# Memory attention: probabilities times values as float32 products that write to one partition half, instead of split products with a fold

## The chip, the cores and the metric

The kernel runs on one core of one Trainium2 chip. The metric is device time in microseconds: the time of the core from start to end of one execution, the median of three runs. The profile is of one further execution, in which each engine's instructions are recorded: PE (matmuls; PEld is its weight load), DVE (VectorE), ACT (ScalarE), POOL (GpSimd), and SP, which issues most DMAs.

## What is computed

Two layers of an encoder on 1024 tokens of width 1024, all in float32. A layer mixes tokens in three groups (Fourier, window attention, memory attention), projects, and runs a SwiGLU block. The change touches the memory attention alone: 4 heads of 64 channels attend to 256 memory rows.

```python
def _memory_attn(q, km, vm):
    b, s, _, _ = q.shape
    scores = jnp.einsum('bshd,bmhd->bhsm', q, km).astype(jnp.float32) * (HEAD_DIM ** -0.5)
    probs = jax.nn.softmax(scores, axis=-1)
    out = jnp.einsum('bhsm,bmhd->bshd', probs.astype(vm.dtype), vm)
    return out.reshape(b, s, MEM_WIDTH)
```

## The kernel before

Operands of most matmuls are split: `split` (lines 149 to 152) writes a rounded copy `hi` (type fp32r, on ACT, line 151) and the rest `lo = src - hi` (on DVE or POOL, line 152), and a product is the sum of hi x hi, hi x lo, lo x hi. A few matmuls take float32 operands directly; one of them is the second half of the window attention (line 773), where two products write to partitions 0 to 63 and 64 to 127 of one tile.

Memory attention in a layer is eight units, one for each of 4 heads and 2 halves of the tokens (512 each). A unit has three steps, and `mem_units` (line 879) runs scores of unit i, values of unit i - 2 and the turn of unit i - 1 together:

- `mem_scores` (829): 16 matmuls `ms` of 256 columns, row maxima on DVE (842), exponentials on ACT (846), the division on POOL (852);
- `mem_turn` (857): 8 transposes `mpT` on PE, and for each of the two blocks of 128 memory rows a `split` of the 128x512 probabilities: one ACT copy and one DVE subtraction;
- `mem_values` (868): 4 matmuls `mav` of 512 columns. The stationary operand holds the head's 64 channels of V twice, the rounded part for partitions 0 to 63 and the rest for 64 to 127, so the tile holds two partial sums. ACT copies one to the head's partition half of `ym` (876), DVE adds the other (877).

`Memory.load` (455) reads K and V of the layer back from DRAM (`kvd`, one DMA), makes the stacked K (`dup_stack`) and splits V.

The program weaves these units with the q projection (`qp`, with the transposes `qT`), and with `load_wout`, which loads 256 KB pieces of the output weights through three buffers (`raws`) and splits each with one ACT (910) and one DVE instruction (911); it needs the buffers of the q weights, so it begins when the q projection ends. After the memory attention come the output product of the Fourier and memory groups (`mo`) and the window attention (`sc`, `pT`, `av`). A scheduler then fixes each engine's order; at run time every engine goes through its own list in that order and waits where an operand is not there.

Of the kernel before, what the change touches and what calls it, by code (L numbers as in the profile page):

```python
# [12 lines left out]
F32R = mybir.dt.float32r  # L13
# [3 lines left out]
ALU = mybir.AluOpType  # L17
# [8 lines left out]
HD = 64  # L26
# [42 lines left out]
def tile_encoder(ctx: ExitStack, tc: tile.TileContext, T, C, out):  # L69
    nc = tc.nc  # L70
# [24 lines left out]
    def shaped(ap, shape):  # L95
        names = "abcde"[: len(shape)]
        dims = {c: d for c, d in zip(names, shape)}
        return ap.rearrange(f"p ({' '.join(names)}) -> p {' '.join(names)}", **dims) if len(shape) > 1 else ap

    def at(k, *shape, dt=F32):  # L100

        o = int(k * 256)
        ap = arenas[F32R if dt is F32R else F32][:, o : o + math.prod(shape)]
        return shaped(ap.bitcast(dt) if dt is I32 else ap, shape)
# [16 lines left out]
    def run(k, n, step):  # L121
        return Ring(*[k + i * step for i in range(n)])
# [9 lines left out]
    ras, rbs, bsums, xs_ = run(40, 3, 2), run(46, 6, 2), Ring(58, 32, 34), Ring(36, 24)  # L132

    zzs, dhs, tabs = run(112, 2, 4), run(64, 2, 4), run(72, 4, 2)
    mps, phs, yys = run(24, 2, 4), run(16, 3, 4), run(104, 2, 4)
    wcs, abs_ = Ring(112, 116, 96, 100, 48, 52, 56, 60), Ring(80)

    def sm(n, name="v"):
# [4 lines left out]
    def ps(shape, name="ps", tag="pd"):  # L143
        return psp[tag].tile([P] + list(shape), F32, tag=tag, name=nm(name))

    f32 = lambda ap: ap.bitcast(F32)
    mm = nc.tensor.matmul

    def split(hi, lo, src, lo_eng=None):

        nc.scalar.copy(hi, src)  # L151
        return (lo_eng or nc.vector).tensor_tensor(out=lo, in0=src, in1=f32(hi), op=ALU.subtract)  # L152
# [16 lines left out]
    def cst(*shape):  # L169
# [20 lines left out]
        out=mask[:, 0:P], in_=mask[:, 0:P], pattern=[[1, P]], compare_op=ALU.is_ge,  # L190
# [4 lines left out]
        out=mask[:, 2 * P : 3 * P], in_=mask[:, 2 * P : 3 * P], pattern=[[-1, P]],  # L195
# [179 lines left out]
    def dup_stack(kh, kl, src, j):  # L375

        r = slice(64 * j, 64 * j + 64)
        o = slice(64 - 64 * j, 128 - 64 * j)
        nc.scalar.copy(kh[r], src[r])
        nc.scalar.copy(kh[o], src[r])  # L380
        nc.vector.tensor_tensor(out=kl[r], in0=src[r], in1=f32(kh[r]), op=ALU.subtract)
        nc.vector.tensor_tensor(out=kl[o], in0=src[r], in1=f32(kh[r]), op=ALU.subtract)
# [9 lines left out]
    class Memory:  # L392
# [60 lines left out]
            nc.sync.dma_start(kvd[self.l], at(self.ks, 1024))  # L453

        def load(self):
            raw = at(32, 4, 256)
            nc.sync.dma_start(raw, kvd[self.l].rearrange("p (i c) -> p i c", i=4))
            self.km = [at(16 + 4 * i, 2, 2, NMEM, dt=F32R) for i in range(2)]
            self.vm = at(120, 2, 4, 2, HD, dt=F32R)
            for ci in range(2):  # L460
                for j in range(2):
                    dup_stack(self.km[ci][:, j, 0], self.km[ci][:, j, 1], raw[:, ci], j)
            v = raw[:, 2:4].rearrange("p t (h d) -> p t h d", h=4)
            for mt in range(2):
                split(self.vm[:, mt, :, 0, :], self.vm[:, mt, :, 1, :], v[:, mt])


    class Mix:
# [388 lines left out]
        def mem_turn(self, e):  # L857
            res = []
            for mt in range(2):
                pT = ps([4, P], "mpT", "pT")  # L860
                for b in range(4):
                    nc.tensor.transpose(pT[:, b, :], e[b // 2][:, b % 2, mt * P : mt * P + P], ident)
                pp = mps(2, 512, dt=F32R)
                split(pp[:, 0], pp[:, 1], pT.rearrange("p h q -> p (h q)"))
                res.append((pp[:, 0], pp[:, 1]))
            return res

        def mem_values(self, h, half, pp):
            av = ps([512], "mav", "av")
            for mt in range(2):  # L870
                lhs = self.mem.vm[:, mt, h].rearrange("p a d -> p (a d)")
                for i in range(2):
                    mm(av, lhs, pp[mt][i], start=mt == 0 and i == 0, stop=mt == 1 and i == 1)
            s = h % 2
            d = self.ym[half][64 * s : 64 * s + 64, h // 2, :]
            nc.scalar.copy(d, av[64:128])
            nc.vector.tensor_tensor(out=d, in0=av[0:64], in1=d, op=ALU.add)

        def mem_units(self):
            todo = [(h, half) for half in range(2) for h in range(4)]  # L880
# [401 lines left out]
    kvd = drp.tile([DEPTH, P, 1024], F32, name="kvd")  # L1282
# [34 lines left out]
    for l in range(DEPTH):  # L1317
# [4 lines left out]
        q = mix.skewed(mix.q, mix.q_turn, NT)  # L1322
# [132 lines left out]
```

## Time and profile before

| | |
|---|---|
| median of 3 runs | 2135.3 us (2132.69 to 2136.14) |
| the profiled execution's own time | 2135.5 us |
| its span, first to last instruction | 2133.7 us |
| busy: PE, DVE, ACT, POOL | 2013.2, 1577.7, 1060.6, 863.4 us |
| mean granted TensorE clock | 0.969 of full |

Busy time is the union of an engine's instructions; a share of the span is an average over stages with different limits, so the stage that changes has to be read by itself. The memory attention lies at about 141 to 228 us (layer 0) and 1200 to 1284 us (layer 1).

### The profile page before, as it was taken

How to read it: one execution, taken by the hardware profiler on the slowest of the kernel's cores; microseconds unless marked ns; L12 is line 12 of the kernel's file. 1: busy time of each engine (PE TensorE's matmuls, PEld its weight loads, DVE VectorE, ACT ScalarE, POOL GpSimd, SP SyncE). 2: the span in 40 equal slices, each digit the busy share in tenths (PEclk: the TensorE clock that was granted, in tenths of full speed). 3: DMA queues.
4: the chain of work that ended last, by engine and by line, in shares of the span. 5: the costliest groups of instructions: out<-in, count | busy, mean ns of one | idle time of the engine just before them, and what ended most of it. 6: DMA issues, size and time to landing. Idle time of an engine off the chain costs nothing.

```text
span 2133.7 us, 28334 instructions
## 1 busy us (share of the span) xinstructions
PE 2013.2 (94%) x9490; PEld 1655.0 (78%) x9490; DVE 1577.7 (74%) x2441; ACT 1060.6 (50%) x2257; POOL 863.4 (40%) x858
## 2 busy tenths in 40 slices
PE   7998999699999999999989989996999999999997
PEld 6887887478888887878868768775888888878785
DVE  7568756898877877657875686578987787876774
ACT  6467776553333334444544677776433333345441
POOL 4244446653423434213453444475442333431322
PEclk9998999899999999999989989998999999999998
DMA  6112123422332326968731122243232232378874
GB/s 221 45 50 65 65 94 105 152 65 94 118 101 95 112 94 194 318 221 287 246 138 41 60 64 85 75 137 110 84 129 94 94 111 92 123 249 284 276 261 138
DMA packets 173602, 287.50 MB, mean 135 GB/s; under 512 B 15480, under 2 KB 73360, under 8 KB 173456
## 3 DMA queue, kind: packets, MB, share of 16 engines
q1 hardware_dynamic: 165392, 266.82, 38.1%
q10 hardware_dynamic: 8064, 18.88, 2.3%
q8 instruction: 74, 1.21, 0.2%
q14 instruction: 72, 0.59, 0.1%
HBM read 219.06 MB, written 66.58 MB: 134 GB/s over the span
## 4 chain that ended last, share of the span: by engine, by line
PE 74%; DMA 8%; DVE 7%; ACT 4%; POOL 4%; issue 2%; SPq 0%; POOLq 0%; DVEq 0%; ACTq 0%
PE fo L1232 12%; PE qz L1104 11%; PE qx L1104 11%; PE qy L1104 11%; PE mo L162 7%; PE qw L1104 5%; PE kvp L162 4%; PE qp L162 3%; DVE arena_r L152 3%; DMA arena_f<-actd 2%; PE sc L728 2%; PE pT L765 2%; DMA arena_f<-in_w_ffn_out 1%; ACT arena_r L151 1%; PE zT L162 1%
## 5 line engine op out<-in xcount | busy, mean ns | idle before, releaser
L151 ACT CAST arena_r<-arena_f 128x512 fp32r<-128x512 f32 (+1 forms) x780 | 443.1, 591 | 674.0 <-PE qz L1104 115.5
L152 DVE TENSOR_TENSOR arena_r<-arena_f,arena_r 128x512 fp32r<-128x512 f32 (+1 forms) x676 | 536.6, 816 | 182.9 <-ACT arena_r L151 179.6
L1232 PE MATMUL fo<-arena_r 128*128 128x512 f32 x1848 | 432.2, 395 | 17.5 <-ACT arena_r L151 15.1
L1232 PEld LDWEIGHTS fo<-arena_r 128*128 128x128 f32 x1848 | 351.7, 191 | 94.6 <-ACT arena_r L151 17.7
L1104 PE MATMUL qy<-arena_r 128*128 128x512 f32 x1056 | 261.5, 397 | 27.6 <-ACT arena_r L151 16.5
L1104 PEld LDWEIGHTS qy<-arena_r 128*128 128x128 f32 x1056 | 201.5, 192 | 72.0 <-ACT arena_r L151 17.0
L1094 DVE TENSOR_TENSOR arena_f<-arena_f 128x512 f32<-128x512 f32 x220 | 206.0, 939 | 5.1
L1104 PE MATMUL qz<-arena_r 128*128 128x512 f32 x704 | 196.3, 389 | 1.8 <-DVE arena_r L152 1.8
L1124 POOL TENSOR_TENSOR arena_f<-arena_f 128x512 f32<-128x512 f32 x44 | 73.0, 1658 | 292.8 <-ACT arena_f L1109 292.8
L1216 POOL TENSOR_TENSOR arena_f<-arena_f 128x512 f32<-128x512 f32 x50 | 73.6, 1475 | 269.5 <-DVE arena_r L152 136.2
L1104 PEld LDWEIGHTS qz<-arena_r 128*128 128x128 f32 x704 | 132.0, 188 | 29.8 <-DVE arena_r L152 2.4
L1156 POOL TENSOR_TENSOR arena_f<-arena_f 128x512 f32<-128x512 f32 x44 | 73.6, 1674 | 165.6 <-DVE arena_f L1136 119.1
L152 POOL TENSOR_TENSOR arena_r<-arena_f,arena_r 128x256 fp32r<-128x256 f32 (+2 forms) x104 | 88.8, 859 | 118.4 <-ACT arena_r L151 93.3
L1104 PE MATMUL qx<-arena_r 128*128 128x512 f32 x528 | 127.7, 389 | 1.4 <-ACT arena_r L151 1.4
L1104 PE MATMUL qw<-arena_r 128*128 128x512 f32 x528 | 127.6, 389 | 0.0
L1104 PE MATMUL qx<-big,arena_r 128*128 128x512 f32 x528 | 126.8, 389 | 0.0
L1104 PEld LDWEIGHTS qx<-arena_r 128*128 128x128 f32 x528 | 99.1, 188 | 22.5 <-ACT arena_r L151 2.0
L1104 PE MATMUL qz<-big,arena_r 128*128 128x512 f32 x352 | 115.5, 389 | 0.0
L1104 PEld LDWEIGHTS qw<-arena_r 128*128 128x128 f32 x528 | 99.1, 188 | 20.8
L1104 PEld LDWEIGHTS qx<-big,arena_r 128*128 128x128 f32 x528 | 99.1, 188 | 20.6
L162 PE MATMUL mo<-arena_r 128*128 128x512 f32 x384 | 102.6, 406 | 5.5 <-POOL arena_r L152 4.0
L162 PE MATMUL mo<-big,arena_r 128*128 128x512 f32 x384 | 102.3, 404 | 0.0
(223 smaller groups left out, 3558.1 us busy)
## 6 DMA issues: line engine op xcount, KB each, us to landing
arena_f<-in_w_ffn_out SPq DMA_DIRECT2D x264, 256.0 KB, 4.3
arena_f<-in_w_ffn_in SPq DMA_DIRECT2D x88, 512.0 KB, 3.6
actd<-arena_f SPq DMA_DIRECT2D x154, 256.0 KB, 3.7
arena_f<-actd SPq DMA_DIRECT2D x154, 256.0 KB, 4.2
arena_f<-in_w_in SPq DMA_DIRECT2D x40, 256.0 KB, 2.7
arena_f<-in_x SPq DMA_DIRECT2D x16, 512.0 KB, 4.1
arena_f<-in_w_out SPq DMA_DIRECT2D x32, 256.0 KB, 2.8
pmd<-arena_f ACTq DMA_DIRECT2D x32, 256.0 KB, 2.0
```

The source lines that it names most:

```text
L151: nc.scalar.copy(hi, src)
L152: return (lo_eng or nc.vector).tensor_tensor(out=lo, in0=src, in1=f32(hi), op=ALU.subtract)
L162: mm(self.dst, a, b, start=self.i == 0, stop=self.i == self.n - 1)
L728: mm(pt, lhs, self.kst[g][i][:, k0 * P : k1 * P], start=i == 0, stop=i == 1)
L765: nc.tensor.transpose(pT[:, h, :], es_[h // 2][:, h % 2, j * P : j * P + P], ident)
L1094: nc.vector.tensor_tensor(out=s, in0=a, in1=b, op=op)
L1104: mm(pt, a, b, start=start and n == 0, stop=n == 11, skip_group_check=not start)
L1124: nc.gpsimd.tensor_tensor(out=self.v, in0=self.v, in1=self.s2, op=ALU.add)
L1156: (G if i in (0, 3) else V).tensor_tensor(out=a[i], in0=c, in1=g[i], op=ALU.mult)
L1216: (nc.vector, nc.gpsimd)[k % 2].tensor_tensor(out=s, in0=x, in1=y, op=op)
L1232: mm(pt, ab[:, 0, x, sl], ab[:, 1, y], start=new and first and j == 0, stop=last and j == 2, skip_group_check=not new)
```

## The change

V stays in float32: `Memory.load` fetches K and V with two DMAs into two places and no longer splits V. `mem_turn` copies each turned block of probabilities once (ACT, float32) into one of four buffers `mps` in place of a split into one of two. `mem_values` makes two float32 products of 64 x 512 a head in place of four split ones of 128 x 512; they write straight to the partition half that the head has in `ym`, and one ACT copy moves it there. What goes: two DVE subtractions and one DVE addition a unit, and V's split (two ACT, two DVE instructions a layer).

```diff
-    mps, phs, yys = run(24, 2, 4), run(16, 3, 4), run(104, 2, 4)
+    mps, phs, yys = Ring(14, 56, 58, 10), run(16, 3, 4), run(104, 2, 4)
...
-            raw = at(32, 4, 256)
-            nc.sync.dma_start(raw, kvd[self.l].rearrange("p (i c) -> p i c", i=4))
+            raw, v = at(32, 2, 256), at(12, 2, 256)
+            kv = kvd[self.l].rearrange("p (i c) -> p i c", i=4)
+            nc.sync.dma_start(raw, kv[:, 0:2])
+            nc.sync.dma_start(v, kv[:, 2:4])
...
-            v = raw[:, 2:4].rearrange("p t (h d) -> p t h d", h=4)
-            for mt in range(2):
-                split(self.vm[:, mt, :, 0, :], self.vm[:, mt, :, 1, :], v[:, mt])
...
-                pp = mps(2, 512, dt=F32R)
-                split(pp[:, 0], pp[:, 1], pT.rearrange("p h q -> p (h q)"))
-                res.append((pp[:, 0], pp[:, 1]))
+                pf = mps(512)
+                nc.scalar.copy(pf, pT.rearrange("p h q -> p (h q)"))
+                res.append(pf)
...
-        def mem_values(self, h, half, pp):
+        def mem_values(self, h, half, pf):
+
+            r = slice(64 * (h % 2), 64 * (h % 2) + 64)
             av = ps([512], "mav", "av")
             for mt in range(2):
-                lhs = self.mem.vm[:, mt, h].rearrange("p a d -> p (a d)")
-                for i in range(2):
-                    mm(av, lhs, pp[mt][i], start=mt == 0 and i == 0, stop=mt == 1 and i == 1)
-            s = h % 2
-            d = self.ym[half][64 * s : 64 * s + 64, h // 2, :]
-            nc.scalar.copy(d, av[64:128])
-            nc.vector.tensor_tensor(out=d, in0=av[0:64], in1=d, op=ALU.add)
+                mm(av[r], self.mem.vm[:, mt, h], pf[mt], start=mt == 0, stop=mt == 1)
+            nc.scalar.copy(self.ym[half][r, h // 2, :], av[r])
```

The scheduler orders all engines anew. First place: PE in layer 0, the second unit's values (`mav_1709` before, `mav_1699` after) among the q projection's matmuls `qp`. Before:

```order
L162 MATMUL qp_1863<-big_1252,arena_r 128x512 x2
L873 MATMUL mav_1709<-arena_r 128x512
L162 MATMUL qp_1863<-big_1252,arena_r 128x512 x2
L840 MATMUL ms_1694<-arena_r 128x256 x4
L873 MATMUL mav_1709<-arena_r 128x512 x3
L862 MATMUL mpT_1716<-const,arena_f 128x128 x3
```

After:

```order
L162 MATMUL qp_1838<-big_1252,arena_r 128x512
L872 MATMUL mav_1699<-arena_f 64x512
L162 MATMUL qp_1838<-big_1252,arena_r 128x512
L872 MATMUL mav_1699<-arena_f 64x512
L162 MATMUL qp_1838<-big_1252,arena_r 128x512 x3
L839 MATMUL ms_1675<-arena_r 128x256 x4
```

Four matmuls of 128 columns out became two of 64, each alone between matmuls of the whole array. The same holds for the third unit, whose two products stand around the last `qp` of the layer.

Second place: DVE in layer 0, just after the q projection, where the weight splits (L911 before, L907 after) run. Before:

```order
L911 SCALAR_TENSOR_TENSOR big_2010<-arena_f,const,big_2010 128x512
L877 TENSOR_TENSOR arena_f<-mav_1794,arena_f 64x512
L152 TENSOR_TENSOR arena_r<-mpT_1801,arena_r 128x512
L152 TENSOR_TENSOR arena_r<-mpT_1808,arena_r 128x512
L843 TENSOR_SCALAR nmx_1768<-rmax_1767 128x2
L842 TENSOR_REDUCE rmax_1815<-ms_1818 128x2
L911 SCALAR_TENSOR_TENSOR big_2010<-arena_f,const,big_2010 128x512
```

After:

```order
L907 SCALAR_TENSOR_TENSOR big_1975<-arena_f,const,big_1975 128x512
L842 TENSOR_SCALAR nmx_1753<-rmax_1752 128x2
L907 SCALAR_TENSOR_TENSOR big_1975<-arena_f,const,big_1975 128x512
L842 TENSOR_SCALAR nmx_1753<-rmax_1752 128x2
L389 TENSOR_TENSOR arena_r<-qT_1866,arena_r 64x4x128
L841 TENSOR_REDUCE rmax_1795<-ms_1798 128x2
```

The two subtractions and the addition of a unit are gone from between the weight splits; nothing else took their place.

Third place: PE in layer 0, the values of the last two units at the end of the memory attention (`sc` and `pT` are the window attention's). Before:

```order
L728 MATMUL sc_2194<-arena_r 128x384 x2
L728 MATMUL sc_2198<-arena_r 128x384 x2
L728 MATMUL sc_2298<-arena_r 128x384 x2
L873 MATMUL mav_2054<-arena_r 128x512
L925 MATMUL ssp_2103<-const,arena_f 128x2 x2
L873 MATMUL mav_2054<-arena_r 128x512 x3
```

After:

```order
L872 MATMUL mav_1989<-arena_f 64x512
L727 MATMUL sc_2143<-arena_r 128x384 x2
L727 MATMUL sc_2147<-arena_r 128x384 x2
L861 MATMUL mpT_1993<-const,arena_f 128x128
L861 MATMUL mpT_1999<-const,arena_f 128x128
L861 MATMUL mpT_1993<-const,arena_f 128x128
L861 MATMUL mpT_1999<-const,arena_f 128x128
L764 MATMUL pT_2120<-const,arena_f 128x128 x4
L872 MATMUL mav_2014<-arena_f 64x512
```

The products of two neighbouring heads, which write to different partition halves, stand apart from each other; nowhere in the list do two heads' products follow one another.

## Rows read from the trace of the kernel before

**Rows 1.** The page: span, then busy time, share and instructions of three engines.

```profile
span 2133.7 us, 28334 instructions
PE 2013.2 (94%) x9490; PEld 1655.0 (78%) x9490; DVE 1577.7 (74%) x2441; ACT 1060.6 (50%) x2257; POOL 863.4 (40%) x858
```

**Rows 2.** Busy time by stretch: length, then PE, PEld, DVE, ACT, POOL, clock, DMA.

```profile
core 0: us, PE busy (x) PEld busy (x) DVE busy (x) ACT busy (x) POOL busy (x), PEclk, DMA share, GB/s
141.00:179.00 38.00, 38.00 (x202) 32.19 (x201) 30.09 (x56) 17.67 (x47) 14.64 (x20) 1.00 0.00 1
180.00:222.00 42.00, 33.05 (x154) 26.36 (x152) 38.88 (x80) 34.74 (x88) 16.14 (x26) 0.80 0.26 82
222.00:230.00 8.00, 7.74 (x29) 6.97 (x30) 3.87 (x17) 5.27 (x19) 3.83 (x7) 0.57 0.00 1
1240.00:1284.00 44.00, 35.99 (x167) 27.15 (x165) 39.72 (x89) 35.93 (x94) 18.61 (x28) 0.84 0.25 78
1284.00:1292.00 8.00, 7.81 (x40) 6.40 (x41) 5.84 (x17) 6.78 (x20) 5.70 (x11) 1.00 0.19 69
```

**Rows 3.** The chain that ended last, 158 to 181 us: start, length, what.

```profile
164.63 5.03 PE qp L162 x22
...
176.54 0.93 PE qp L162 x4
177.47 0.23 PE mav L873
...
178.63 0.71 PE mav L873 x3
...
179.37 0.59 ACT arena_f L876
...
179.97 1.02 ACT arena_f L846 x4
```

**Rows 4.** Line 773's float32 matmuls: count, shortest, median and longest ns.

```profile
L773 PE MATMUL av<-big,arena_f x176: 379/379/431, 306.7 to 1440.9; 128*64 128x256 f32 x176
```

**Rows 5.** Timeline of PE around line 773: start, length, count of records.

```profile
306.40 0.40 PE L162 MATMUL mo<-arena_r 128*128 128x512 f32 x1
306.73 0.44 PE L773 MATMUL av<-big,arena_f 128*64 128x256 f32 x2
...
306.73 0.65 PE L773 MATMUL av<-big,arena_f 128*64 128x256 f32 x4
...
307.00 0.39 PE L773 MATMUL av<-big,arena_f 128*64 128x256 f32 x2
307.31 0.27 PE L925 MATMUL ssp<-const,arena_f 128*128 128x2 f32 x1
...
323.71 1.08 PE L773 MATMUL av<-big,arena_f 128*64 128x256 f32 x8
```

**Rows 6.** Busy time by stretch of the instructions on `mpT`: PE, PEld, DVE, ACT.

```profile
180.00:222.00 42.00, 8.11 (x42) 5.98 (x40) 7.85 (x12) 6.65 (x12) 0.80 0.26 82
1240.00:1284.00 44.00, 8.57 (x40) 5.66 (x40) 8.06 (x12) 6.65 (x12) 0.84 0.25 78
```

**Rows 7.** The same for line 877, DVE alone.

```profile
180.00:222.00 42.00, 4.08 (x6) 0.80 0.26 82
1240.00:1284.00 44.00, 4.18 (x7) 0.84 0.25 78
```

**Rows 8.** What SP's queue waited for, 100 to 230 us: total, times, longest.

```profile
SPq L909 <- DVE big L911: 57.2, 8, 47.5
```

**Rows 9.** The load of K and V, and the group with V's rounded copies.

```profile
L457 SPq DMA_DIRECT2D arena_f<-kvd x2: 339/339/339, 97.7 to 1160.0; - x2
...
DMA to landing us min/median/max: 3.2/3.2/3.2
...
L151 ACT CAST arena_r<-arena_f 128x256 fp32r<-128x256 f32 x84 | 33.2, 404 | 25.5 <-PE mo L162 10.3 <-PE ms L840 5.8 <-PE yfp L162 3.8
```

More of the change, by code (lines that the diff above doesn't have):

```diff
@@ L455, in load @@
         def load(self):
-            raw = at(32, 4, 256)
-            nc.sync.dma_start(raw, kvd[self.l].rearrange("p (i c) -> p i c", i=4))
+            raw, v = at(32, 2, 256), at(12, 2, 256)
+            kv = kvd[self.l].rearrange("p (i c) -> p i c", i=4)
+            nc.sync.dma_start(raw, kv[:, 0:2])
+            nc.sync.dma_start(v, kv[:, 2:4])
             self.km = [at(16 + 4 * i, 2, 2, NMEM, dt=F32R) for i in range(2)]
-            self.vm = at(120, 2, 4, 2, HD, dt=F32R)
+            self.vm = v.rearrange("p t (h d) -> p t h d", h=4)
             for ci in range(2):
```

## The prediction, made before the changed kernel was run

> **What bounds the kernel now.** The page comes first: PE is busy for 2013.2 of 2133.7 us, DVE for 1577.7, ACT for 1060.6 [rows 1]. By that alone, work taken from DVE is worth nothing. But the memory attention is only two stretches of some 85 us, so the second view is busy time by stretch, cut there. It shows two regimes in each layer. From 141 to 179 us PE is busy for all of 38.00 us at full clock and DVE for 30.09: the q projection runs there, and two units' values lie among its matmuls. From 180 to 222 us the picture turns over: DVE is busy for 38.88 of 42.00, ACT for 34.74, PE for 33.05 at a mean granted clock of 0.80, a mix of its 1.2 and 2.4 GHz levels. Layer 1 repeats it at 1240 to 1284 us: DVE 39.72 of 44.00, ACT 35.93, PE 35.99 at 0.84 [rows 2]. The third view, the chain that ended last, confirms the border: up to 179.3 us every link is PE, and then it goes over to ACT (the copy L876, the exponentials L846) [rows 3]. So the change is read twice: what PE pays in the first stretch, where everything waits for it, and what DVE gives back in the second, where it is the fullest engine.
>
> **What a head costs PE.** Now: four matmuls of 512 columns. The chain gives 22 of that size 5.03 us, 0.229 each, and three `mav` 0.71 [rows 3], so a head is 0.92 us. The new products, float32 with 64 columns out, are not in the memory attention's trace, but line 773 has the form with 256 columns. Its 176 records belong to 88 products (22 key blocks a layer, two halves, two layers), so a product is two records [rows 4]. Eight records take 1.08 us, four 0.65 [rows 5]: four more, that is one product to each partition half, add 0.43. There are two readings. If the two halves run side by side, each product takes the whole 0.43 for 256 columns, 0.86 for 512. If the records run one after another, a product is 0.22 for 256 and 0.43 for 512. In a window of 20 ns the timeline already shows two records begun at 306.73 [rows 5], where one after another would put 0.11 between them; I take 0.86 and keep 0.43 as the lower end.
>
> Going over to such a matmul and back costs too: from the last `mo` at 306.40 to the first record at 306.73 is 0.33 where 0.23 is usual, and from the last pair at 307.00, which streams for 0.215, to the next matmul at 307.31 another 0.10 is lost [rows 5]. A head with both products together is then 2 x 0.86 + 0.2 = 1.92 us, and 2.12 where other matmuls stand between them, as at the first place of the order. Against 0.92 that is 1.0 to 1.2 more, 1.1 in the mean; by the lower reading 0.14 to 0.34.
>
> One rule of the skill would make this cheaper. Line 773's pairs start together [rows 5], but in the new order two heads' products nowhere stand side by side. The Trainium skill, TensorEngine Tiling (Array Packing), section Key Properties, says that different tiles of the array can load weights and multiply in parallel. By that rule a pair of neighbouring heads would cost what one does, if the order brought them together; it does not, so the sum goes without it, and it stands below as a rival.
>
> **The first stretch: a loss.** In the new order the first two units' values lie among the `qp` as before, and the third's two products stand around the last of them. PE has no gap there. Two heads at 1.1 and half of the third make 2.8 us a layer, 5.6 in all. By the lower reading it is 1.2; with the third in full and split, 1.0 + 1.2 + 1.2 = 3.4 a layer, 6.8.
>
> **The second stretch: a gain.** DVE loses the subtractions, 7.85 us in layer 0 and 8.06 in layer 1 [rows 6], and the additions, 4.08 and 4.18 [rows 7]: 11.9 of its 38.88 and 12.2 of its 39.72. It falls to 27 and 27.5 and bounds no more. Next is ACT, whose copies stay as many and as large: 34.74 and 35.93. DVE as the bound filled 0.926 and 0.903 of the stretches. If ACT does as well, the stretches shrink to 34.74 / 0.926 = 37.5 and 35.93 / 0.903 = 39.8 us: gains of 4.5 and 4.2. What can keep ACT below that is its supply of output weights: SP's loads L909 waited for DVE's L911 for 57.2 us in total [rows 8] (47.5 of it in one wait, for the end of the q projection), and a DVE that comes sooner to L911 frees those buffers sooner. The two pull against each other, so I take the same shares, 8.7 in all. Bounds: nothing, if another engine fills the stretch; at ACT 0.95, 5.4 and 6.2, 11.6 in all.
>
> **The clock.** From 222 to 230 us PE is busy for 7.74 of 8.00 at a clock of 0.57, while the same place of layer 1 (1284 to 1292) has 1.00 [rows 2]. Before that, PE had stood idle for 9 of 42 us. Most of these 8 us are work at half speed, about 3.3 us lost. A shorter stretch with more matmuls in it leaves PE less idle and may spare this; I count half, 1.7 us, between nothing and 3.3.
>
> **Edits at nothing.** V's split goes, two ACT copies of 0.40 [rows 9] and two DVE subtractions a layer, in the first stretch behind a full PE. The load is cut in two; V's part now stands in SP's queue behind three loads of q weights, of which the last issues before 134 us, and the one load of before took 3.2 us to land [rows 9], while the first values stand at about 170 us: 30 us of cover. V and two of the four new buffers lie where the window attention's output goes, so its first copy waits for the last head's products; PE's list has them before that output's own matmuls anyway. Four buffers in place of two only take waits away.
>
> **The sum**, against the profiled execution's own 2135.5 us (0.2 above the median of the runs): + 5.6 - 8.7 - 1.7 = - 4.8, so 2130.7; I say 2131.
>
> **The rivals.** A difference of 0.2%, 4.3 us, is about what a measurement of this kernel tells from none.
>
> *PE becomes the bound of the second stretch: slower.* Its busy time there times the clock is 33.05 x 0.80 = 26.4 us at full speed, and five or six heads at 1.1 add 6.1: 32.5. At the old clock that needs 40.6 of 42 us; in layer 1, (30.2 + 6.1) / 0.84 = 43.2 of 44. The gain is then 1.4 + 0.8, the loss the full 6.8, and the time 2140. It decides below a clock of 0.83 in layer 0, where PE alone needs over 39.2 us and the gain no longer covers 2.8. For it: six heads at half clock would hold up the `ms` behind them for nearly 4 us each. Against: an engine with more to do stood at full clock in every full stretch [rows 2]. The Trainium skill, TensorE: Matmul & The Clock Gate, section Part 1, likewise says that the clock follows how busy the array has been. Chance 0.22.
>
> *ACT fills the stretch at 0.87 only*, because it also waits for weights and for PE's longer products: gains of 2.1 and 2.7 less 5.6, time 2136. No change. Chance 0.29.
>
> *All goes well:* ACT at 0.95 and the clock spared, + 5.6 - 11.6 - 3.3 = - 9.3, time 2126; the lower reading of the product's cost, 4.4 less than the sum, gives 2126 too. Chance 0.14 together.
>
> *Two heads overlap*, by the rule on tiles: each pair in the first stretch would give back one head, 1.9 us, 3.8 in all: 2127. The order speaks against it. Chance 0.03. That the change doesn't do what it says is ruled out by the order, where the DVE instructions are gone.
>
> **How the numbers follow.** My own case has 0.32, most of it just over the bound of 4.3 us: 0.27 faster, 0.05 same. Faster: 0.27 + 0.14 + 0.03 = 0.44; same 0.05 + 0.29 = 0.34; slower 0.22. The range goes from the good case less 2 us, 2124, to PE's rival plus 1, 2141; my case's own is 2128 to 2134.
>
> **What would show it.** Right: in the profile after, `mav` has 32 products of 512 columns as 64 records that follow each other at about 0.43 us; the first stretch is 2 to 4 us longer, all PE; in the second DVE falls to about 27 us, ACT leads the chain, and the stretch is 3 to 5 us shorter. Wrong: PE's clock falls further in the second stretch and the chain goes through `mav` there; or records follow at 0.22; or the order around the window attention opens a new gap on PE after 230 us.

## The result and the profile after

The changed kernel takes 2138.8 us in the median (2134.8 to 2144.9, 20 runs) against 2133.7 before (2127.3 to 2136.4, 20 runs): a ratio of 1.0027, 95% interval [1.002, 1.0034], by which it is about 5.8 us slower. The forecast was 2131, from a sum of -4.8 us. The profiled execution has a span of 2138.7 us.

The page of the changed kernel, span and busy time, where [rows 1] stand for before:

```profile
span 2138.7 us, 28251 instructions
PE 2023.1 (95%) x9490; PEld 1642.3 (77%) x9490; DVE 1565.7 (73%) x2389; ACT 1059.3 (50%) x2253; POOL 858.9 (40%) x858
```

PE has 10 us more, DVE 12 us less. The second stretches alone were to give some 24 us of DVE back, so other instructions of DVE took longer; one kind of them is shown below. The stretches of [rows 2], with the same columns:

```profile
141.00:179.00 38.00, 38.00 (x191) 30.33 (x190) 25.45 (x49) 18.92 (x50) 14.03 (x19) 1.00 0.00 1
180.00:222.00 42.00, 35.66 (x161) 21.29 (x160) 27.73 (x61) 33.69 (x89) 19.12 (x31) 0.96 0.26 82
222.00:230.00 8.00, 7.87 (x39) 5.00 (x39) 5.26 (x19) 5.39 (x12) 0.86 (x3) 1.00 0.00 0
1240.00:1284.00 44.00, 37.17 (x153) 21.13 (x152) 27.08 (x57) 33.56 (x83) 16.56 (x26) 0.88 0.26 78
1284.00:1292.00 8.00, 7.89 (x45) 6.54 (x45) 5.53 (x24) 7.84 (x26) 3.77 (x8) 1.00 0.10 34
```

DVE fell to 27.7 and 27.1 us, as forecast. The clock did not fall but rose, from 0.80 to 0.96 and from 0.84 to 0.88, and the 8 us at 0.57 now stand at 1.00. Yet ACT, which was to fill 0.926 and 0.903 of these stretches, fills 33.69 / 42 = 0.80 and 33.56 / 44 = 0.76. In layer 0 this window begins 9 us before the last `qp` of the changed kernel, so here are the second stretches at its own borders, from the last `qp` to the last `mav`:

```profile
189.00:227.00 38.00, 31.63 (x137) 17.39 (x137) 26.59 (x59) 31.31 (x81) 15.36 (x27) 0.96 0.28 91
1246.00:1284.00 38.00, 31.17 (x124) 16.94 (x124) 24.26 (x51) 28.36 (x69) 14.30 (x23) 0.87 0.29 90
```

There ACT fills 0.82 and 0.75, PE 0.83 and 0.82. No engine is full.

What a head costs PE is in three views. First the float32 products by tile, where [rows 4] gave the form that they were priced by (count, then shortest, median and longest ns):

```profile
L872 PE MATMUL mav<-arena_f x64: 592/593/1116, 168.9 to 1283.5; 128*64 128x512 f32 x64
```

Then the timeline of PE (start, length, records), where [rows 5] showed line 773:

```profile
166.82 2.20 PE L162 MATMUL qp<-big,arena_r 128*128 128x512 f32 x9
168.95 1.93 PE L872 MATMUL mav<-arena_f 128*64 128x512 f32 x4
170.81 1.21 PE L162 MATMUL qp<-big,arena_r 128*128 128x512 f32 x4
...
178.57 1.07 PE L872 MATMUL mav<-arena_f 128*64 128x512 f32 x2
179.58 0.49 PE L162 MATMUL qp<-big,arena_r 128*128 128x512 f32 x1
180.00 1.07 PE L872 MATMUL mav<-arena_f 128*64 128x512 f32 x2
```

And the chain, where [rows 3] showed that of before (start, length, what):

```profile
164.00 5.01 PE qp L162 x22
169.02 1.86 PE mav L872 x4
170.88 1.14 PE qp L162 x4
...
178.64 1.00 PE mav L872 x2
179.65 0.43 PE qp L162
180.07 1.00 PE mav L872 x2
```

The 64 records belong to 32 products. By the timeline a head whose products stand together takes 1.93 us, one that is split 2 x 1.07. These spans overlap a little with the matmuls around them; what the chain pays, from one start to the next, is 1.86 and 2.00. The prices of the forecast were 1.92 and 2.12. Behind 179 us the chain of before went over to ACT; now it stays with PE until 192 us.

Of the smaller views, SP's wait of [rows 8] is still there, and the loads of [rows 9] are two (the lines of the waits of SP's queue, and of the load's two sources):

```profile
SPq L905 <- DVE big L907: 57.1, 5, 50.2
...
SPq L459 <- DVE arena_r L152: 6.1, 1, 6.1
```

```profile
L458 SPq DMA_DIRECT2D arena_f<-kvd x2: 338/338/339, 98.3 to 1157.6; - x2
...
L459 SPq DMA_DIRECT2D arena_f<-kvd x2: 327/327/327, 121.9 to 1180.9; - x2
```

V lands at about 125 us; its first product begins at 168.95, so V's own load holds nobody up.

### The profile page after: what moved, and what is told of

Read it like the earlier page. It is cut to its first block, busy times and chain, and to the rows that moved or that the text cites. A ratio compares the mean times of both kernels' runs of the same rounds, so it can differ in the third digit from the quotient of the medians.

```text
span 2138.7 us, 28251 instructions
## 1 busy us (share of the span) xinstructions
PE 2023.1 (95%) x9490; PEld 1642.3 (77%) x9490; DVE 1565.7 (73%) x2389; ACT 1059.3 (50%) x2253; POOL 858.9 (40%) x858
## 4 chain that ended last, share of the span: by engine, by line
PE 75%; DVE 8%; DMA 7%; ACT 4%; POOL 3%; issue 3%; SPq 0%; DVEq 0%; POOLq 0%; ACTq 0%
PE fo L1228 13%; PE qz L1100 11%; PE qx L1100 11%; PE qy L1100 11%; PE mo L162 6%; PE qw L1100 5%; PE qp L162 4%; PE kvp L162 4%; DVE arena_r L152 3%; DMA arena_f<-actd 2%; PE sc L727 1%; PE pT L764 1%; PE mav L872 1%; PE zT L162 1%; DMA arena_f<-in_w_ffn_out 1%
## 5 line engine op out<-in xcount | busy, mean ns | idle before, releaser
L151 ACT CAST arena_r<-arena_f 128x512 fp32r<-128x512 f32 (+2 forms) x776 | 442.3, 592 | 681.9 <-PE qz L1100 121.0
L152 DVE TENSOR_TENSOR arena_r<-arena_f,arena_r 128x512 fp32r<-128x512 f32 x672 | 539.2, 824 | 170.8 <-ACT arena_r L151 167.8
L1100 PE MATMUL qy<-arena_r 128*128 128x512 f32 x1056 | 264.4, 400 | 25.7 <-ACT arena_r L151 18.7
L1100 PEld LDWEIGHTS qz<-arena_r 128*128 128x128 f32 x704 | 132.2, 188 | 27.7 <-DVE arena_r L152 0.3
```

The lines of the kernel that those rows point to most:

```text
L1100: mm(pt, a, b, start=start and n == 0, stop=n == 11, skip_group_check=not start)
```

## The experiments

All are read by one table, the length of each part of the program in one profiled execution. The borders are starts of matmuls: the first `ms` of layer 0 (in layer 1 the first `kvp`, the key and value projection of the window attention, since some orders move work between the two), the last `qp`, the last `mav`, and the first `fo` of the layer's SwiGLU output. "First" ends with the last `qp`, "second" with the last `mav`, "behind" with the first `fo`; "between" goes from there to layer 1, "end" from there to the end of the span. Each ratio is to executions of before that were timed beside that kernel's. For instance, the tile `mav` of the changed kernel in layer 0, and `qp` there (first and last start are the two times):

```profile
L872 PE MATMUL mav<-arena_f x32: 592/592/1116, 168.9 to 226.3; 128*64 128x512 f32 x32
```

```profile
L162 PE MATMUL qp<-big,arena_r x192: 387/389/504, 130.1 to 189.3; 128*128 128x512 f32 x192
```

so its second stretch in layer 0 is 226.3 - 189.3 = 37.0 us.

| kernel | first 0 | second 0 | behind 0 | between | first 1 | second 1 | behind 1 | end | median us | ratio to before, 95% interval |
|---|---|---|---|---|---|---|---|---|---|---|
| before | 44.4 | 39.6 | 618.0 | 264.0 | 138.0 | 37.6 | 610.4 | 240.7 | | |
| e6_null_before | 44.4 | 39.0 | 617.4 | 263.1 | 137.5 | 36.1 | 610.1 | 240.4 | 2132.2 | 0.9994 [0.9981, 1.0006] |
| after | 47.4 | 37.0 | 613.6 | 265.9 | 140.3 | 37.4 | 618.3 | 236.9 | 2138.8 | 1.0027 [1.0020, 1.0034] |
| e7_null_after | 47.3 | 35.9 | 613.4 | 264.9 | 141.5 | 37.4 | 618.1 | 240.9 | 2139.8 | 1.0022 [1.0007, 1.0037] |
| e1_no_dve | 44.6 | 36.4 | 613.6 | 267.6 | 135.9 | 34.2 | 618.4 | 241.6 | 2129.5 | 0.9987 [0.9978, 0.9997] |
| e2_dve_back | 48.3 | 41.1 | 616.9 | 262.1 | 139.8 | 39.6 | 621.2 | 238.1 | 2158.3 | 1.0121 [1.0101, 1.0141] |
| e4_load_cut | 43.9 | 41.0 | 615.0 | 262.3 | 134.8 | 39.2 | 621.4 | 240.8 | 2140.4 | 1.0037 [1.0024, 1.0051] |
| e9_rounded | 44.1 | 32.0 | 617.4 | 266.0 | 137.2 | 33.4 | 621.5 | 239.7 | 2132.5 | 0.9995 [0.9985, 1.0005] |
| e5_one_load | 47.6 | 36.0 | 613.3 | 262.4 | 135.4 | 38.2 | 612.4 | 240.9 | 2132.5 | 0.9993 [0.9980, 1.0005] |
| e10_k_place | 47.3 | 35.4 | 613.5 | 263.2 | 135.5 | 39.8 | 613.0 | 239.1 | 2131.6 | 0.9990 [0.9980, 0.9999] |
| e3_pair | 45.0 | 29.6 | 615.6 | 261.7 | 136.3 | 31.5 | 621.6 | 238.4 | 2123.3 | 0.9967 [0.9954, 0.9980] |
| e11_pair_k_place | 46.6 | 37.5 | 614.5 | 263.6 | 134.0 | 39.0 | 605.0 | 238.7 | 2123.9 | 0.9955 [0.9939, 0.9972] |
| e12_pair_01 | 46.6 | 35.0 | 613.4 | 264.2 | 139.3 | 32.4 | 619.5 | 237.9 | 2132.0 | 1.0001 [0.9988, 1.0014] |
| e13_pair_both | 45.0 | 29.7 | 615.7 | 264.4 | 131.6 | 32.1 | 614.3 | 240.4 | 2118.6 | 0.9932 [0.9916, 0.9948] |

Two theories were put to it: theory 1, that the dearer products cost PE more than DVE's relief gives; theory 2, that the time is lost in stages that the edit does not touch, through the order that the scheduler writes for them.

### Relief alone, and price alone: e1_no_dve, e2_dve_back, e9_rounded

The relief without the price, on the kernel before:

```diff
-                split(pp[:, 0], pp[:, 1], pT.rearrange("p h q -> p (h q)"))
-                res.append((pp[:, 0], pp[:, 1]))
+                nc.scalar.copy(pp[:, 0], pT.rearrange("p h q -> p (h q)"))
+                res.append((pp[:, 0], pp[:, 0]))
...
-            nc.scalar.copy(d, av[64:128])
-            nc.vector.tensor_tensor(out=d, in0=av[0:64], in1=d, op=ALU.add)
+            nc.scalar.copy(d, av[0:64])
```

> The kernel before without VectorE's work on the probabilities' rests and without its addition of the two halves of each head; TensorE keeps its four split products a head. The rests of the probabilities and of the products' low halves are left out of the result. Theory 1 (the float32 products cost TensorE more than the relief of VectorE gives): the relief alone, without the dearer products, is a gain, 4 to 9 us, so 2125 to 2130 where before stands at 2134. Theory 2 (the loss is the order that the scheduler makes of everything behind the change, and not the change's own work): the time moves by up to 5 us either way, without relation to the work taken out; a loss here would speak for it, and then the memory attentions' own stretches would be shorter while later stretches are longer.

The price without the relief, on the changed kernel:

```diff
...
                 nc.scalar.copy(pf, pT.rearrange("p h q -> p (h q)"))
+                nc.vector.tensor_tensor(out=rests(512, dt=F32R), in0=pT.rearrange("p h q -> p (h q)"), in1=pf, op=ALU.subtract)
...
-            nc.scalar.copy(self.ym[half][r, h // 2, :], av[r])
+            d = self.ym[half][r, h // 2, :]
+            nc.scalar.copy(d, av[r])
+            nc.vector.tensor_tensor(out=rests(512, dt=F32R)[r], in0=av[r], in1=d, op=ALU.subtract)
```

> The changed kernel with VectorE's work put back as plain load: one subtraction for each turned block and one for each head, into buffers that nobody reads. Theory 1: the relief that this change did give (4 to 9 us) is lost again, so slower than the changed kernel: 2142 to 2148, ratio to before 1.004 to 1.007. If VectorE's relief gave nothing because the second stretch waits for TensorE anyway: 2138 to 2140, as the changed kernel. Theory 2: within 5 us of the changed kernel on either side, with the differences in stretches that hold no memory attention.

And both the relief and a cheap product:

```diff
...
-            self.vm = v.rearrange("p t (h d) -> p t h d", h=4)
+            self.vm = at(120, 2, 4, 2, HD, dt=F32R)
+            for i in range(2):
+                nc.scalar.copy(self.vm[:, :, :, i, :], v.rearrange("p t (h d) -> p t h d", h=4))
...
-                pf = mps(512)
+                pf = mps(512, dt=F32R)
...
-                mm(av[r], self.mem.vm[:, mt, h], pf[mt], start=mt == 0, stop=mt == 1)
+                mm(av, self.mem.vm[:, mt, h].rearrange("p a d -> p (a d)"), pf[mt], start=mt == 0, stop=mt == 1)
```

> The changed kernel with its products on operands rounded to fp32r, two of 512 columns a head, so that TensorE pays less than half of before and VectorE's relief stays; the rests of probabilities and values are left out of the result. Theory 1: this takes 1.5 us of TensorE per head from the changed kernel, 12 a layer, and both memory attentions become shorter than before by 5 to 10 us each; if the stretches fell by less than 3 us, TensorE's price would not be what held ScalarE back. Total 2120 to 2128. Theory 2 adds up to 8 us on either side from the stages behind.

In total, e1 stands at 2129.5, by its ratio a gain of 2.8 us where 4 to 9 were expected; e2 came to 2158.3, beyond all that was expected (its profiled execution was its fastest, at 2151.0, so the table explains only that one; the rest stays open); e9 came to before's time, far short of its gain. The parts tell more. Beside the mean of two executions of one order (before and e6: 39.3 and 36.9 in the second stretches), e1's relief gives 2.9 and 2.7 us there. With the products dear, taking the same DVE work away gives 41.1 to 36.5 (mean of after and e7) and 39.6 to 37.4. And e9, with the cheap product, gives 7.3 and 3.5, where 5 to 10 were expected in each layer.

These sizes are sure to some 2.5 us only. The lists of e11 and e12 (below) are the same on PE, DVE, ACT and POOL until layer 1, and their second stretches in layer 0 still took 37.5 and 35.0 us; e4 (below), which takes no work away, has 41.0 and 39.2. What doesn't hang on such sizes is what ACT waited for. Here are its waits in the second stretches alone (total, times, longest), from 189 to 227 and from 1246 to 1284 us in the changed kernel those for the product:

```profile
ACT arena_f L873 <- PE mav L872: 0.8, 2, 0.4
...
ACT arena_f L873 <- PE mav L872: 3.9, 3, 3.3
```

In e1, from 185 to 222 us the two largest, and from 1239 to 1274 us those for weights and for the product:

```profile
ACT arena_r L909 <- DMA arena_f<-in_w_out: 1.9, 2, 0.9
ACT big L909 <- DMA arena_f<-in_w_out: 1.7, 1, 1.7
...
ACT big L909 <- DMA arena_f<-in_w_out: 1.7, 1, 1.7
...
ACT arena_r L909 <- DMA arena_f<-in_w_out: 1.0, 1, 1.0
...
ACT arena_f L876 <- PE mav L873: 0.5, 1, 0.5
```

So the dear product costs ACT 0.8 us in layer 0 and 3.9 in layer 1, against none listed and 0.5 in e1, which has the old product. (Summed over 141 to 1292 us the changed kernel's wait is 18.1 us, but 12.4 of that lie in the first stretches, where ACT is not what the time hangs on.) The long wait in layer 1 has the clock in it:

```profile
1262.85 3.68 PE L872 MATMUL mav<-arena_f 128*64 128x512 f32 x4 [1.90 <-ACT arena_f L863]
...
1276.76 1.97 PE L872 MATMUL mav<-arena_f 128*64 128x512 f32 x2
```

```profile
1262.00:1267.00 5.00, 4.15 (x6) 1.30 (x7) 1.76 (x4) 4.78 (x14) 2.34 (x4) 0.50 0.41 120
```

From 1262 to 1267 us the granted clock was 0.50, the 1.2 GHz level, and a head took 3.68 us in place of 1.93. ACT's single wait of 3.3 us ends at 1280.4, behind the half head that took 1.97 in place of 1.07. e7, the same list once more, has 3.67, 1.97 and a wait of 3.2.

But even with PE at its old price ACT does not come near 0.926. The second stretches of e1, cut at its own borders:

```profile
185.00:222.00 37.00, 27.82 (x142) 21.16 (x142) 29.81 (x69) 31.57 (x83) 13.82 (x23) 0.91 0.30 93
1239.00:1274.00 35.00, 27.80 (x131) 21.73 (x129) 25.01 (x55) 29.55 (x76) 13.91 (x22) 0.80 0.30 96
```

ACT fills 0.853 and 0.844. What it waited for most was the output weights, 3.6 us in layer 0 and 2.7 in layer 1: the supply that the prediction named and charged nothing for. All three kernels, e4 too, lose 8 to 11 us in "behind 1", where none of their edits lies.

### The load cut in two: e4_load_cut, e5_one_load, e10_k_place

One part of the change alone, made in the kernel before:

```diff
-            raw = at(32, 4, 256)
-            nc.sync.dma_start(raw, kvd[self.l].rearrange("p (i c) -> p i c", i=4))
+            raw, v = at(32, 2, 256), at(12, 2, 256)
+            kv = kvd[self.l].rearrange("p (i c) -> p i c", i=4)
+            nc.sync.dma_start(raw, kv[:, 0:2])
+            nc.sync.dma_start(v, kv[:, 2:4])
...
```

> The kernel before with one part of the change alone: the load of keys and values cut into two transfers; the values are still split. Theory 1: within 0.2% of before, 2132 to 2136, since the transfer is waited for by nobody near the end of the chain. Theory 2: the small change in order moves the time by more than 0.2% although no work changed.

It cost as much as the whole change and a little more: 1.0037. On its face this says that the load, costed at nothing, is the culprit. So it was undone in the changed kernel:

```diff
-            raw, v = at(32, 2, 256), at(12, 2, 256)
-            kv = kvd[self.l].rearrange("p (i c) -> p i c", i=4)
-            nc.sync.dma_start(raw, kv[:, 0:2])
-            nc.sync.dma_start(v, kv[:, 2:4])
+            raw = at(10, 4, 256)
+            nc.sync.dma_start(raw, kvd[self.l].rearrange("p (i c) -> p i c", i=4))
+            v = raw[:, 2:4]
```

> The changed kernel with one part undone: keys and values come in one transfer again, values still float32. The cut of the load alone, made in the kernel before, cost 7.2 us. Theory 2 (the order that the scheduler makes of the rest): that 7.2 is no cost of the load, so undoing it does not give 7 us back; the time is anywhere within 6 us of the changed kernel, 2133 to 2145. Rival (the cut load itself costs 7 us, by its place in the queue of transfers): 2131 to 2133.

6 us came back, the rival's number. But this edit also gave the keys another place, and with it the list of layer 1 became that of before: of the 900 matmuls from the end of its memory attention into the next SwiGLU block, the last 768 stand in before's order, where in the changed kernel's list not even the last ones agree. The next kernel tells the two apart, with the load left in two and only the place changed:

```diff
-            raw, v = at(32, 2, 256), at(12, 2, 256)
+            raw, v = at(10, 2, 256), at(12, 2, 256)
```

> The changed kernel with the keys loaded to another free place; the load stays cut in two, and no work changes. The scheduler's order of layer 1 behind the memory attention becomes that of the kernel before. Theory 2 (what is lost behind the memory attention hangs on the order alone): that part of layer 1, 276.5 us in the changed kernel against 268.6 before, falls to 268 to 272, and the whole to 2131 to 2135. Rival (the cut load costs the time): as the changed kernel, 2137 to 2140.

2131.6: one number, no work, and the changed kernel's loss is gone. Its list shares the same 768 matmuls with before's. Theory 2's reading holds and the rival's falls: a load in two costs nothing by itself. Nor does the place: the lists of PE, DVE, ACT and POOL are the changed kernel's until layer 1, and layer 0's "first", "second" and "behind" come out as in e7 within 0.5 us, though the keys' load there starts at 129.3 us in place of 98.3. In layer 1, "behind 1" went from 618.3 to 613.0 and "first 1" from 140.3 to 135.5, while "second 1" rose from 37.4 to 39.8. The stretch behind by windows, in the changed kernel and in e10, both from the end of the memory attention into the next SwiGLU block:

```profile
1284.00:1560.00 276.00, 254.12 (x1302) 203.97 (x1302) 211.24 (x412) 171.53 (x412) 146.50 (x170) 0.97 0.28 96
```

```profile
1278.00:1549.00 271.00, 251.85 (x1302) 203.36 (x1303) 204.71 (x411) 172.67 (x412) 140.46 (x170) 0.97 0.30 98
```

The same 1302 records, in 276 us by the one order and 271 by the other; PE is busy for 2.3 us more and idle for 2.7 more, DVE busy for 6.5 more. Here the first rows in which the two kernels' PE lists part, in layer 1's q projection (- changed kernel, + e10):

```
 L162 MATMUL qp_9684<-big_9630,arena_r 128x512 x3
 L162 MATMUL qp_9712<-big_9630,arena_r 128x512 x3
+L162 MATMUL yfp_9644<-arena_r 128x256 x6
 L162 MATMUL qp_9684<-big_9630,arena_r 128x512 x2
+L162 MATMUL qp_9684<-big_9637,arena_r 128x512
 L162 MATMUL qp_9712<-big_9630,arena_r 128x512 x2
-L162 MATMUL yfp_9644<-arena_r 128x256 x6
```

From one group of Fourier matmuls set elsewhere, the difference goes on to 461 rows of PE's list.

Part of what the order does can be seen on DVE. `nmx`, a small instruction of the window attention, took 0.518 us in the mean behind the changed kernel's memory attention and 0.222 in e10 (busy time, mean ns and idle time before it stand behind the bar):

```profile
L734 DVE SCALAR_TENSOR_TENSOR nmx<-rmax,const 128x4 f32<-128x4 f32 x16 | 8.3, 518 | 0.4
```

```profile
L734 DVE SCALAR_TENSOR_TENSOR nmx<-rmax,const 128x4 f32<-128x4 f32 x15 | 3.3, 222 | 0.3
```

With no POOL instruction beside it, one takes 0.15 to 0.16 us. The longest ones began while POOL was at work and ended with POOL's instruction, and ACT waited for them; in the changed kernel:

```profile
1421.57 2.83 POOL L325 TENSOR_TENSOR arena_f<-arena_f 128x1024 f32<-128x1024 f32 x1
...
1422.08 2.34 DVE L734 SCALAR_TENSOR_TENSOR nmx<-rmax,const 128x4 f32<-128x4 f32 x1
...
1424.45 0.62 ACT L740 ACTIVATE arena_f<-arena_f,nmx 128x384 f32<-128x384 f32 x1 [3.07 <-DVE nmx L734]
```

`nmx` makes up 5.0 of the 6.5 us that DVE is busy for longer. How much of the time that layer 1 loses hangs on them is not shown.

### Edits that change no work: e6_null_before, e7_null_after

V's two blocks split in the other order (before), and V loaded before K (after):

```diff
-            for mt in range(2):
+            for mt in (1, 0):
                 split(self.vm[:, mt, :, 0, :], self.vm[:, mt, :, 1, :], v[:, mt])
```

```diff
-            nc.sync.dma_start(raw, kv[:, 0:2])
             nc.sync.dma_start(v, kv[:, 2:4])
+            nc.sync.dma_start(raw, kv[:, 0:2])
```

> The kernel before with an edit that changes no work at all: the two blocks of the values are split in the other order. Theory 2: the scheduler's order of the rest differs again and the time moves by up to 8 us, more likely up than down, since the kernel before lost 8 to 11 us in layer 1's window attention in every variant so far. Theory 1 (only the work of an edit counts): 2133, within 0.1%.

> The changed kernel with its two loads in the other order, values first: no work changes. Theory 1: 2138 to 2140, as the changed kernel. Theory 2: it moves by up to 6 us on either side; in both the two memory attentions last as long as in the changed kernel, within 2 us each.

Theory 2 expected movement from e6 and there was none: not every edit shakes the order. Its lists came out the same as before's on every engine, and e7's the same as the changed kernel's but on SP. That makes them repeats. "Behind 0" and "behind 1" repeat within 0.6 us, most parts within 1.5, "end" within 4.0 (a second stretch can differ by more, as e11 and e12 showed). Differences of 5 to 11 us behind the memory attention belong to the order and not to chance.

### Two heads at once: e3_pair, e12_pair_01, e11_pair_k_place, e13_pair_both

The products of two neighbouring heads are issued next to each other, and one copy moves both (on the changed kernel):

```diff
...
-            r = slice(64 * (h % 2), 64 * (h % 2) + 64)
             av = ps([512], "mav", "av")
-            for mt in range(2):
-                mm(av[r], self.mem.vm[:, mt, h], pf[mt], start=mt == 0, stop=mt == 1)
-            nc.scalar.copy(self.ym[half][r, h // 2, :], av[r])
+            for mt in (1, 0):
+                for s in (1, 0):
+                    mm(av[64 * s : 64 * s + 64], self.mem.vm[:, mt, h + s], pfs[s][mt], start=mt == 1, stop=mt == 0)
+            nc.scalar.copy(self.ym[half][:, h // 2, :], av)
...
-                if i >= 2:
-                    h, half = todo[i - 2]
+                if i >= 3 and i % 2:
+                    h, half = todo[i - 3]
...
-                    self.mem_values(h, half, pp.pop(i - 2))
+                    self.mem_values(h, half, (pp.pop(i - 3), pp.pop(i - 2)))
```

> The changed kernel with the products of two neighbouring heads issued next to each other, into the two halves of one bank, and one copy for both on ScalarE. If products on different column halves run beside each other: a pair costs TensorE about 1.9 us in place of 3.8, and its four products show as one group of about 1.9 us. Theory 1: TensorE's price is gone and the relief stays, so faster than before by 4 to 8 us: 2126 to 2130. If column halves do not run beside each other: the group takes 3.5 to 3.8 us, and the time is that of the changed kernel less 1 us for the copies saved, 2136 to 2140. Theory 2: any time within 5 us of before, even where the group shows 1.9 us.

2123.3, a ratio of 0.9967, below the 2126 to 2130 of theory 1: the first kernel with the whole work in it that clearly beats both. The timeline of PE in e3:

```profile
190.11 1.94 PE L872 MATMUL mav<-arena_f 128*64 128x512 f32 x8 [1.05 <-ACT arena_f L863]
...
208.41 1.94 PE L872 MATMUL mav<-arena_f 128*64 128x512 f32 x8 [0.35 <-ACT arena_f L863]
```

Eight records, two heads, take 1.94 us, what one head took alone. The Trainium skill, TensorEngine Tiling (Array Packing), section Key Properties, says that tiles of the array can work in parallel; these rows agree. With that the first stretch of layer 0 is back at 45.0, the second ones fall by about 10 and 5 us, and ACT reaches what the forecast had wanted of it, in layer 0 at least:

```profile
187.00:217.00 30.00, 23.07 (x130) 15.47 (x129) 24.77 (x55) 27.50 (x75) 14.16 (x21) 0.94 0.32 97
1230.00:1262.00 32.00, 23.75 (x128) 15.50 (x126) 24.48 (x53) 27.55 (x71) 14.44 (x22) 0.89 0.30 91
```

27.50 / 30 = 0.917, and 0.861. "Behind 1" took 11 us back. The next two kernels issue the first block first (the edit against e3); e11 has the keys at the other place as well:

```diff
-            for mt in (1, 0):
-                for s in (1, 0):
-                    mm(av[64 * s : 64 * s + 64], self.mem.vm[:, mt, h + s], pfs[s][mt], start=mt == 1, stop=mt == 0)
+            for mt in (0, 1):
+                for s in (0, 1):
+                    mm(av[64 * s : 64 * s + 64], self.mem.vm[:, mt, h + s], pfs[s][mt], start=mt == 0, stop=mt == 1)
```

> The products of two neighbouring heads next to each other as in the first pair kernel, issued first block first, and the keys at the other place. Its order behind the second memory attention is that of the kernel before. Theory: the pair's gain in the two memory attentions (15 us in the first pair kernel) stays, and the 11 us that the first pair kernel lost behind the second one shrink to 2 to 4: 2114 to 2119, faster than both kernels. If the order behind does not matter: 2122 to 2125, as the first pair kernel.

> The same pair kernel with the keys at their place in the changed kernel; the order behind the second memory attention is another than before's. Theory: the memory attentions last as long as in the run beside it within 2 us, and the part of layer 1 behind is 275 to 281 us: 2121 to 2127. If the order does not matter: the same time as the run beside it.

The half on the order held: e11's "behind 1" is 605.0, e12's 619.5, 14.5 us between them. The half on the pair failed: in layer 0 both lost more than half of its gain (second stretch 37.5 and 35.0 against e3's 29.6 and before's 39.3), in layer 1 e11 lost all of it (39.0) and e12 kept most (32.4). So both missed their ranges, e12 with 2132.0 where 2121 to 2127 was expected. In e12 the products do not stay together:

```profile
191.96 1.93 PE L872 MATMUL mav<-arena_f 128*64 128x512 f32 x6 [1.12 <-ACT arena_f L863]
...
202.25 1.07 PE L872 MATMUL mav<-arena_f 128*64 128x512 f32 x2 [0.78 <-ACT arena_f L863]
...
207.55 1.93 PE L872 MATMUL mav<-arena_f 128*64 128x512 f32 x6
```

The first block's probabilities are ready earlier, so the scheduler puts a product ahead alone, where it has no partner: 1.07 + 1.93 a pair in place of 1.94. Layer 1 of e12 has such pairs too and yet kept most of the gain, so this is not all of it. Last block first, all four are ready at once in the second stretches. So the last kernel takes e3 with the keys at the other place:

```diff
-            raw, v = at(32, 2, 256), at(12, 2, 256)
+            raw, v = at(10, 2, 256), at(12, 2, 256)
```

> The first pair kernel (last block first, where all four products of two heads stand in one group of 1.94 us) with the keys at the other place. By what the group does: layer 0's memory attention stays 8 to 10 us shorter than before, and layer 1's, taken from the start of its key and value projections, at least 6 shorter. The order behind the second one is neither that of before nor that of the first pair kernel, so that part is open: 264 to 280 us. Whole: 2114 to 2126; below 2121 it beats every kernel so far.

2118.6, ratio 0.9932 [0.9916, 0.9948]: the best of all, 14.5 us faster than before by the ratio.

## Why the prediction was wrong

By the table, each kernel as the mean of two executions of its order (before and e6, after and e7), the differences add up to 8.2 us, where the ratio gives 5.8: the execution of e6 that was profiled, 2130.2 us, lies below that kernel's median of 2132.2.

- **The first stretch** was right in layer 0: a loss of 2.8 us forecast, 2.95 measured, and all of it PE's: up to the last `qp` the chain has one head at 1.86, one at 2 x 1.00 and half of a third at 1.00, where before it had two at 0.92 and a matmul. The price of a head was right to about 0.1 us. In layer 1 the 3.15 measured is in part luck: e5 and e10, with the same products in another order, have 135.4 and 135.5 there, less than before.
- **The second stretch** is the step that failed: a gain of 8.7 and 1.7 for the clock was forecast, 2.85 - 0.55 = 2.3 came. The assumption "ACT does as well as DVE" did not hold, in two ways. The relief alone (e1) gave 5.6, not 8.7: with PE at its old price ACT filled 0.853 and 0.844 and waited for output weights, which the sum charged nothing for. And the price of the other heads, which the sum charged nowhere either, took back 3.3 more, nearly all in layer 1 (34.2 to 37.4): each head's products stand between ACT's copy of the probabilities and ACT's copy of the product, and there ACT waited 3.9 us for them against 0.5, most of it behind a product at the low clock. How the 2.3 divides into these two is sure only to some 2.5 us, by the spread above; that the whole is far below 10.4 is sure, since e5 and e10, with the same products, have 2.0 and 1.0.
- **The clock** went as hoped from 222 to 230 us, and for most of the second stretch in layer 0; in layer 1 it fell to 0.50 around some of the products. What it is worth shows in layer 0, where the same list ran four times: 37.0 us at 0.96 in the changed kernel, 35.4 to 36.0 at 1.00 in e5, e7 and e10: about 1 us, if the clock is all that made them differ. The prediction's "an engine with more to do stood at full clock in every full stretch" did not hold in its own rows: from 222 to 230 us PE was busy for 7.74 of 8.00 at 0.57. The Trainium skill, TensorE: Matmul & The Clock Gate, section Part 1, says that the clock follows how busy the array has been. From the kernel before to the changed one the stretches go that way, with PE at 33.05 and then 35.66 of 42 us; e9's does not, with 22.08 of 33 at 0.95, so the busy share of a whole stretch does not tell its clock here:

```profile
186.00:219.00 33.00, 22.08 (x123) 17.13 (x121) 24.12 (x56) 29.05 (x73) 15.87 (x26) 0.95 0.29 90
```

- **PE as the bound**, the slower rival, had the right side and nearly the right time, 2140, by luck: PE was to be the fullest engine at the old clock, and it fills 0.83 at 0.96. Its remark that a head at half clock takes nearly 4 us was borne out, with 3.68.
- **ACT at 0.87**, the rival of no change, came nearest in the second stretch: e1 shows that fill. It had 4.8 as the gain.
- **Edits at nothing** were right for what they cost themselves (e10), but the sum held the rest of the program still, and it is not: "behind 0" gained 4.2 us and "behind 1" lost 8.0, together 3.8 that no term had. This decides the sign; the prediction's last sign of being wrong, a new gap on PE after 230 us, points there without a price. With another order and the same work (e10), the change is 0.9990 of before, [0.9980, 0.9999], about 2 us faster and no difference that counts.
- **Two heads overlap** was a right rule, put aside because the order kept them apart; e3 brings them together.

From -4.8 to +8.2 are 13.0 us: 8.1 of too large a gain in the second stretch, 3.8 of order, and 1.1 in "first", "between", "end" and the 0.5 before them. Why layer 1 runs better by before's order than by the changed kernel's stays open but for the longer DVE instructions: PE is busy and idle for longer by the worse one, which was seen and not explained.

## What to carry to other kernels

Relieving the fullest engine of a stretch gives what the next chain of waits allows, not the next engine's busy time: price what stands between that engine's own instructions, here weights that had not landed and PE's product between two ACT copies. Read waits in the stretch that counts: summed over more, most of ACT's wait for the product lay where nothing hung on it. Products with 64 output columns pay when two of them, for the two column halves, become ready together and stand side by side in the list. And where a scheduler writes the order, measure an edit in its own stretch and again with another order of the rest, since an edit that moves no work (a buffer's place) moved this kernel by 7 us.

## What was not expected of the hardware

Four products of 512 columns onto alternating column halves, eight records, took 1.94 us, the same as two onto one half (1.93). A single one cut off from its partners cost 1.07. At a granted clock of 0.50 a head took 3.68. A DVE instruction on 128x4 elements took 2.34 us beside a long one of POOL, and 0.16 alone. Of one order, parts of 600 us repeat within about 1 us, while whole executions of one kernel, where there are ten or more, spread over 7 to 15 us.
